# Down projection of a transformer step on one core: two of seven half-size products each replaced by seven quarter-size products

## The chip, the cores and the metric

The kernel runs on one core of one Trainium2 chip, as a single launch. The metric is the device time of one execution in microseconds (us), taken as the median of several runs. Engines are called as the profile calls them: PE (TensorE matmul), PEld (its weight loads), DVE (VectorE), ACT (ScalarE), POOL (GpSimd), and SP (SyncE), which here only issues DMAs. Each engine works its own instructions in the order in which the program lists them.

## The reference

One layer of a streaming encoder with 1024 + 32 frames of width 1024: gated mixers (window attention and short convolution), cross-attention, and a squared-ReLU MLP, then a final norm. The change concerns the last product of the MLP and some sums of its weights:

```
def trunk_layer(x, attn_core, conv_left, mem_k, mem_v, ...):
    h = rms_norm(x, g_mix)
...
    x = x + (jax.nn.sigmoid(ga) * a + jax.nn.sigmoid(gb) * bo) @ w_mix_out
...
    x = x + co @ w_co
    hm = rms_norm(x, g_mlp)
    x = x + jnp.square(jax.nn.relu(hm @ w_up)) @ w_down
    return x, k, v, up[:, -(CONV_WIDTH - 1):]
```

`w_down` is 4096 x 1024, so the down product is 1056 frames x 4096 x 1024.

## The kernel before

All data are float32. A product is made in three matmuls: every operand is split into a rounded part `hi` and a rest `lo`, and PE adds `wh*hi + wh*lo + wl*hi`. A weight tile (128 x 1024, 512 KB) is loaded by SP into a raw buffer `wr`, cast to `wh` by ACT, and `wl = wr - wh` is made by DVE (`split`, `issue_w`). There are two `wr` buffers in the down part of the program and three each of `wh` and `wl`; `next_w` keeps two weights ready beyond the one in use. So the load of a weight can start only when DVE has finished the `wl` of the weight two before it.

Activations lie transposed, 128 features to a tile row. The frames are cut into two halves of 528 (`HT`), each of two quarters of 264 (`QT`). The down product is one level of a Strassen-type scheme: seven half-size products named `b11`, `b21`, `n4`, `t2`, `n3`, `n1`, `b22` in that order (`KINDS`), each 528 frames by 2048 by 512. Their operands (sixteen tiles of 128 x 528 each) were written to DRAM by the up part. `stage` runs one such product as eight items (`steps`, or `paired` for `b11`): an item is one weight tile, half of the depth (8 blocks of 128) for one block of 128 outputs, on both quarters, hence 2 x 8 x 3 = 48 matmuls of 264 columns. After an item, `pump2(3)` splits the operand tiles of the next product that have landed (ACT cast, DVE subtraction in `split_here`, L1319 and L1320) and has SP load three more. When a block of outputs is complete, `to_x1` (L1793) adds it from PSUM to the resident activations `x1`, once for each output quadrant that the product contributes to, in three pieces for each quadrant; for `b11` these are twelve DVE additions.

The sums of weights that Strassen products need (`w_sum`, `g_sum`, the up sums) are made earlier, beside attention: `sum_step` has POOL load a piece of 512 KB, make four additions of 128 x 256 (L735), and store it to DRAM. Two tiles alternate. It works through 50 pieces. Operands marked `pin` keep their program order on an engine; the rest is placed by a scheduler at build time.

Of the kernel before, what the change touches and what calls it, by code (L numbers as in the profile page):

```python
# [40 lines left out]
def hybrid_step(ctx: ExitStack, tc: tile.TileContext, io):  # L41
# [44 lines left out]
    wsum_d = dram.tile([4, 2, 4, P, 4, 256], F32, name="wsum_d")  # L86

# [44 lines left out]
    def weight(key):  # L132
        name, *at = key
        if name in ("w_down", "w_sum"):
            q, j, t = at
            return (wsum_d if name == "w_sum" else io[name])[j, t, :, :, q].rearrange("i p c -> p i c")
        if name == "g_sum":
# [572 lines left out]
    pieces += [("u", i, q) for i in range(2) for q in range(2)]  # L710

# [5 lines left out]

    def sum_step():
        old = W.pop("new", None)
        if pieces:  # L720
            at = pieces.pop(0)
            t = sum_tile(len(pieces))
            if at[0] in ("g", "u"):
                kind, f, q = at
                for e in range(2):
                    src = io["w_in"][34 + 8 * e + f] if kind == "g" else io["w_up"][UP[f][e]]
                    src = src.rearrange("p (h c) -> p h c", h=2)
                    pin(pool_e.dma_start(t[:, 2 * e : 2 * e + 2], src[:, :, 256 * q : 256 * q + 256]))
            else:
                pin(pool_e.dma_start(t, io["w_down"][at]))  # L730
            W["new"] = at, t
        if old:
            at, t = old
            for to, x, y in ((3, 2, 3), (2, 0, 2), (0, 0, 3), (1, 1, 0)):
                pin(pool_e.tensor_tensor(t[:, to], t[:, x], t[:, y], op=ALU.add))  # L735
            if at[0] in ("g", "u"):
                kind, f, q = at
                for w in range(2):
                    pin(pool_e.dma_start((gsum_d[f - 1] if kind == "g" else usum_d[f])[:, w, :, 256 * q : 256 * q + 256], t[:, 2 * w : 2 * w + 2]))
            else:  # L740
                pin(pool_e.dma_start(wsum_d[at], t))
# [9 lines left out]
    for i, h in enumerate(hosts):  # L751
# [14 lines left out]
        if i % 2 and i > 1 or i > 3:  # L766
            extras.append((1, sum_step))
        if h[0] == "Q":
# [475 lines left out]
    def open_first():  # L1244

        closed(m_cm)
        S["l"] = ctx.enter_context(tc.tile_pool(name="first", bufs=4, reuse_waits="tile"))
        S["z"] = ctx.enter_context(tc.tile_pool(name="second", bufs=8, reuse_waits="tile"))
# [7 lines left out]
    def open_sums():  # L1256
        closed(cr_cm)
        closed(Y["cm", 1])
        S["s"] = ctx.enter_context(tc.tile_pool(name="sums", bufs=8, reuse_waits="tile"))
        for kind in ("t2", "n1", "n3", "n4"):  # L1260
            for k in range(4):
                comb[kind, k] = tuple(slot(S["s"], kind, HT) for _ in range(2))
# [11 lines left out]
    def open_second():  # L1274
# [3 lines left out]
        S["b"] = ctx.enter_context(tc.tile_pool(name="b22", bufs=8, reuse_waits="tile", side="right"))  # L1278
        L["cm2"], L["pool2"] = opened("late2", bufs=1, reuse_waits="tile", side="right")
        ps = ctx.enter_context(tc.tile_pool(name="ps2", bufs=1, space=PSUM, reuse_waits="tile"))  # L1280

    def zslot(dt=F32R):
        return S["z"].tile([P, HT], dt, tag="Z", name=nm("Z"))

    def lslot(dt=F32):
        return S["l"].tile([P, HT], dt, tag="lt", name=nm("lt"))
# [102 lines left out]
    def second_b22():  # L1389
        for k in range(4):  # L1390
            comb["b22", k] = tuple(slot(S["b"], "b22", HT) for _ in range(2))
# [212 lines left out]
    KINDS = ["b11", "b21", "n4", "t2", "n3", "n1", "b22"]  # L1604

    def dslots(kind, k):
        if KINDS.index(kind) % 2 == 0:
            tag = ("t2", "n1", "n3", "b22")[k // 4]
            pool = S["b" if tag == "b22" else "s"]
            return tuple(slot(pool, tag, HT) for _ in range(2))  # L1610
        if k < 4:
            return tuple(slot(S["s"], "n4", HT) for _ in range(2))
        if k < 8:
            return tuple(zslot() for _ in range(2))
        if k < 10:
            return tuple(lslot(F32R) for _ in range(2))
        return tuple(slot(S["h"], "H", HT) for _ in range(2))

    def pump2(n):
# [3 lines left out]
        for kind, k in wanted2[:n]:  # L1623
            hi, lo = dn[kind, k] = dslots(kind, k)
            sp.dma_start(lo.bitcast(F32), op_d[kind][:, k])
            coming2.append((hi, lo))
        del wanted2[:n]

    def open_down():
# [3 lines left out]
        S["h"] = ctx.enter_context(tc.tile_pool(name="hpool", bufs=12, reuse_waits="tile"))  # L1633
# [154 lines left out]
    def to_x1(h, f, banks, add=True, last=False):  # L1788
        for c, at, q, frm in SEGS[h]:
# [3 lines left out]
            (dve.tensor_add if add else dve.tensor_sub)(*((x, a, x) if add else (x, x, a)))  # L1793
# [79 lines left out]

    def stage(kind, w, then, q=None, each=None, more=None):
        nxt = KINDS.index(kind) + 1
        if nxt < len(KINDS):
            item(lambda: wanted2.extend((KINDS[nxt], k) for k in range(16)))
        for n, (j, t) in enumerate(paired if kind == "b11" else steps):

            def fn(ws, j=j, t=t):  # L1880
                prod(kind, j, t, then, q)(ws)
                pump2(3)
# [10 lines left out]

    stage("b11", ("w_down", 0), ((*A12, True, False), (*A21, False, False), (*A22, False, False), (*A11, True, False)))
    stage("b21", ("w_down", 1), ((*A11, True, True),))
    stage("n4", ("w_down", 3), ((*A21, True, False),))
# [126 lines left out]
```

## Time and profile before

| | |
|---|---|
| time, median of 3 runs (lowest to highest) | 1748.98 us (1746.13 to 1750.31) |
| span of the profiled execution, first to last instruction | 1747.8 us |
| the execution's own time beyond its span | not recorded apart; the median is 1.2 us above the span |
| mean granted PE clock | 0.995 |
| HBM traffic | 346.60 MB moved, mean 198 GB/s |
| the `b11` product | 1400.6 to 1453.2 us, with the tail of the up part in it |
| the six later down products | 46.8 to 47.8 us each |

The profile gives for each engine the time that it was busy; times count from the first instruction. In a list of waits, a row names who waited, for whom, the total, how often, and the longest. In a table by windows, a row gives for one stretch its length, the busy time of each engine with its count of instructions, the granted clock, the busy share of the DMA engines and the GB/s they moved. In lists of one tile's instructions, three numbers are the shortest, median and longest duration in ns. In a timeline, a row starts with start and duration of a run of instructions of one kind.

### The profile page before, as it was taken

Reading aid. Unit: us, or ns where it says so; the run is one execution under the profiler, and the core shown is the slowest. Engines: PE = TensorE matmul, PEld = TensorE weight load, DVE = VectorE, ACT = ScalarE, POOL = GpSimd, SP = SyncE. Lnnn points to the kernel's source line nnn. Section 1 sums busy time; section 2 is a strip of 40 time slices with the busy share of each in tenths; the row PEclk is TensorE's granted clock in tenths of the full one; section 3 lists DMA queues with packets and bytes.
Section 4 is the critical chain, followed back from the end, with each engine's and each line's share of the span. In section 5 each row is a group of like instructions: output and inputs, shape, how many; then the busy total and the mean of one; then the engine's idle time right before and its main releaser. Section 6 shows DMA issues by size and latency. Waiting matters only on the chain. (4 is left out here: it accounts for less than half of the span.)

```text
span 1747.8 us, 32606 instructions
## 1 busy us (share of the span) xinstructions
PE 1727.7 (99%) x12262; PEld 1712.4 (98%) x12262; DVE 1188.1 (68%) x2276; ACT 852.9 (49%) x1660; POOL 586.2 (34%) x667
## 2 busy tenths in 40 slices
PE   9999999999999999999999999999999999999998
PEld 8999999999999999999999999999999999999998
DVE  7776777768666646555677888787666686545675
ACT  8653534535335324434556666765444463332444
POOL 0026366443553544432224232005555410000121
PEclk9999999999999999999999999999999999999999
DMA  4333344333436888867766667775666695555554
GB/s 185 104 126 128 114 134 153 115 139 127 160 132 204 296 292 280 291 203 238 264 213 198 221 227 241 235 258 191 217 222 219 219 330 185 188 193 169 192 170 160
DMA packets 179854, 346.60 MB, mean 198 GB/s; under 512 B 18657, under 2 KB 101249, under 8 KB 179569
## 3 DMA queue, kind: packets, MB, share of 16 engines
q1 hardware_dynamic: 163504, 290.07, 50.0%
q0 software_dynamic: 15568, 53.68, 8.8%
q8 instruction: 96, 1.57, 0.4%
q10 hardware_dynamic: 624, 0.77, 0.1%
q14 instruction: 62, 0.50, 0.1%
HBM read 250.73 MB, written 93.14 MB: 197 GB/s over the span
## 5 line engine op out<-in xcount | busy, mean ns | idle before, releaser
L129 ACT CAST wh<-wr 128x1024 fp32r<-128x1024 f32 (+1 forms) x214 | 223.8, 1046 | 366.6 <-PE acc L1810 121.4
L130 DVE TENSOR_TENSOR wl<-wr,wh 128x1024 fp32r<-128x1024 f32 (+1 forms) x214 | 275.0, 1285 | 106.2 <-ACT wh L129 105.4
L200 PE MATMUL acc<-X,wh 128*128 128x384 f32 (+1 forms) x864 | 281.5, 326 | 0.0
L201 PE MATMUL acc<-X,wh 128*128 128x384 f32 (+1 forms) x864 | 278.8, 323 | 0.1
L202 PE MATMUL acc<-X,wl 128*128 128x384 f32 (+1 forms) x864 | 277.8, 322 | 0.0
L276 POOL TENSOR_TENSOR xacc<-xacc,ct 128x384 f32<-128x384 f32 (+1 forms) x56 | 75.6, 1354 | 379.9 <-ACT ct L274 378.1
L201 PEld LDWEIGHTS acc<-X,wh 128*128 128x128 f32 x864 | 162.7, 188 | 1.7 <-DVE X L280 0.7
L200 PEld LDWEIGHTS acc<-X,wh 128*128 128x128 f32 x864 | 162.4, 188 | 0.8
L202 PEld LDWEIGHTS acc<-X,wl 128*128 128x128 f32 x864 | 162.4, 188 | 0.1
L200 PE MATMUL acc<-Y,wh 128*128 128x384 f32 (+1 forms) x432 | 139.9, 326 | 3.2 <-DVE ct L1068 2.9
L202 PE MATMUL acc<-Y,wl 128*128 128x384 f32 (+1 forms) x432 | 140.0, 325 | 2.7 <-DMA wl<-wl_d 2.7
L201 PE MATMUL acc<-Y,wh 128*128 128x384 f32 (+1 forms) x432 | 139.7, 324 | 0.0
L129 ACT CAST PTh<-pt 128x512 fp32r<-128x512 f32 (+3 forms) x94 | 45.8, 516 | 112.8 <-PE pt L598 111.4
L1809 PE MATMUL acc<-n,wh 128*128 128x264 f32 x352 | 100.2, 285 | 0.0
L1810 PE MATMUL acc<-n,wh 128*128 128x264 f32 x352 | 100.1, 284 | 0.0
L1811 PE MATMUL acc<-n,wl 128*128 128x264 f32 x352 | 99.9, 284 | 0.0
L735 POOL TENSOR_TENSOR ws<-ws 128x256 f32<-128x256 f32 x100 | 89.5, 895 | 5.6
L735 POOL TENSOR_TENSOR xacc<-xacc 128x256 f32<-128x256 f32 x100 | 86.8, 868 | 5.7 <-DMA xacc<-in_w_in 0.4
L200 PEld LDWEIGHTS acc<-Y,wh 128*128 128x128 f32 x432 | 81.4, 189 | 4.4 <-DVE ct L1068 3.8
L202 PEld LDWEIGHTS acc<-Y,wl 128*128 128x128 f32 x432 | 81.5, 189 | 3.0 <-DMA wl<-wl_d 3.0
L201 PEld LDWEIGHTS acc<-Y,wh 128*128 128x128 f32 x432 | 81.6, 189 | 0.0
L584 ACT ACTIVATE S<-S,nmx 128x257 f32<-128x257 f32 (+1 forms) x132 | 64.2, 488 | 18.9 <-DVE nmx L579 17.6
(432 smaller groups left out, 5554.9 us busy)
## 6 DMA issues: line engine op xcount, KB each, us to landing
wr<-in_w_up SPq DMA_DIRECT2D x53, 512.0 KB, 4.5
wr<-in_w_in SPq DMA_DIRECT2D x52, 512.0 KB, 3.6
wr<-wsum_d SPq DMA_DIRECT2D x40, 512.0 KB, 3.5
wr<-in_w_conv_out SPq DMA_DIRECT2D x24, 512.0 KB, 3.9
wr<-in_w_mix SPq DMA_DIRECT2D x24, 512.0 KB, 5.2
wr<-in_w_down SPq DMA_DIRECT2D x24, 512.0 KB, 3.6
n_d<-Z SPq DMA_DIRECT2D x32, 264.0 KB, 4.2
xacc<-in_w_down POOLq DMA_DIRECT2D x16, 512.0 KB, 4.5
```

The source lines that it names most:

```text
L129: act.copy(hi, src)
L130: dve.tensor_sub(lo, src, hi.bitcast(F32))
L200: pe.matmul(out, wh[:, a], hi, start=(k == 0), stop=False)
L201: pe.matmul(out, wh[:, a], lo, start=False, stop=False)
L202: pe.matmul(out, wl[:, a], hi, start=False, stop=(k == len(acts) - 1))
L276: pool_e.tensor_tensor(acc, acc, sq, op=ALU.add)
L584: act.activation(stl[:, h, : nk + 1], stl[:, h, : nk + 1], AF.Exp, scale=-1.0, bias=nmx[:, h : h + 1], accum_out=den[:, h : h + 1],)
L735: pin(pool_e.tensor_tensor(t[:, to], t[:, x], t[:, y], op=ALU.add))
L1809: pe.matmul(a, wh[:, s], hi, start=(t == 0 and k == 0), stop=False, skip_group_check=True)
L1810: pe.matmul(a, wh[:, s], lo, start=False, stop=False, skip_group_check=True)
L1811: pe.matmul(a, wl[:, s], hi, start=False, stop=(t == 1 and k == 7), skip_group_check=True)
```

## The change

**Products.** `b21` and `n4` no longer run as one half-size product each. `stage2` makes each by seven quarter-size products P1 to P7 (264 frames by 1024 by 256), each as two items, one for each block of 128 outputs, written P1.0 and P1.1. An item is one weight tile and 8 x 3 = 24 matmuls of 264 columns. Before, either product had eight items of 48 matmuls; now it has fourteen of 24, in the program's order P1, P6, P2, P7, P5, P4, P3. Each item needs a weight tile of its own: of `w_down` for P1, P2, P4, and of the new sums `w2_d` for P6, P7, P5, P3. Partial results are kept in three pairs of PSUM banks, which alternate from product to product (`into`), and in plain tiles of SBUF (`wide`): ACT copies P1, DVE adds P1 to P6 and P7, and the outputs of P5, P4, P3 get that sum on DVE and are added to `x1` by POOL.

**Operands.** The sums of operands are made in the stage before (`prepare`): the first eight tiles' quarters (`first_sums` on POOL, `first_split`), and the sums `e` (`extra_split`); in the stage itself those of `f` and the split of the last eight tiles (`second_split2`, three of them with POOL's subtraction). The order of the products becomes b11, b21, t2, n4, n3, n1, b22, and the stages around a `stage2` run in the `paired` order. Each 528-column slot has a fixed place and a list of free places decides which tile goes where.

**Weight sums.** Sixteen pieces are added to `sum_step` (66 instead of 50), with 14 more calls beside attention, and the load of the next piece is issued between the second and the third addition instead of ahead of the first.

```
-    KINDS = ["b11", "b21", "n4", "t2", "n3", "n1", "b22"]
+    KINDS = ["b11", "b21", "t2", "n4", "n3", "n1", "b22"]
+    after2 = [KINDS[KINDS.index(kind) + 1] for kind in RAW2]
...
+    pieces += [("w2", kind, i, b) for kind in RAW2 for i in range(2) for b in range(4)]
...
     def sum_step():
+
         old = W.pop("new", None)
...
+        for n, (to, x, y) in enumerate(((3, 2, 3), (2, 0, 2), (0, 3, 0), (1, 1, 0))):
+            if n == 2 and pieces:
+                sum_load()
+            if old:
+                at, t = old
+                op = ALU.subtract if at[0] == "w2" and to != 3 else ALU.add
+                pin(pool_e.tensor_tensor(t[:, to], t[:, x], t[:, y], op=op))
         if old:
...
+        if i % 2 and i > 4:
+            extras.append((2, sum_step))
...
+        order = ("P1", "P6", "P2", "P7", "P5", "P4", "P3")
+        into = {"P1": "A", "P2": "A", "P6": "B", "P7": "B", "P4": "B", "P5": "C", "P3": "C"}
...
+        def beside(n):
+            if n < 2:
+                last_sums(kind, 2 * n)
+                last_sums(kind, 2 * n + 1)
+            if n < 4:
+                second_split2(kind, 2 * n, False)
+                second_split2(kind, 2 * n + 1, n > 0)
+            elif n < 6:
+                last_split(kind, 2 * n - 8)
+                last_split(kind, 2 * n - 7)
+            if n == 5:
+                wanted2.extend((nxt, k) for k in range(16))
+            if n >= 5:
+                pump2({5: 2, 7: 2, 9: 2, 11: 2, 13: 4}.get(n, 0))
...
-    stage("b21", ("w_down", 1), ((*A11, True, True),))
-    stage("n4", ("w_down", 3), ((*A21, True, False),))
+    stage2("b21", *A11, True)
     stage("t2", ("w_sum", 0), ((*A12, False, False), (*A21, True, False), (*A22, True, False)))
+    stage2("n4", *A21, False)
```

How the instructions now stand is shown at three places, all in the `b21` product.

On DVE, where `b11` ends, this stood before (L1793 is an addition of `b11`'s last block to `x1`, `wl` the rest of a weight, here of the third and fourth of `b21`):

```order
L1793 TENSOR_TENSOR Ga_1727_9917<-acc_3078_17544,Ga_1727_9917 128x264
L1793 TENSOR_TENSOR Ga_1727_9917<-acc_3078_17544,Ga_1727_9917 128x120
L1793 TENSOR_TENSOR Gb_1951_10869<-acc_3078_17544,Gb_1951_10869 128x144
L130 TENSOR_TENSOR wl_17739<-wr_17736,wh_17738 128x1024
L130 TENSOR_TENSOR wl_17803<-wr_17800,wh_17802 128x1024
```

On DVE at the same place after the change (L1907 is that addition, L1713 the split of an operand sum `e`, L1356 that of an operand tile; `wl_17933` is the third weight of `b21`, that of P6.0, and `wl_17978` that of P6.1):

```order
L1907 TENSOR_TENSOR Gb_1967_10999<-acc_3104_17709,Gb_1967_10999 128x144
L1713 TENSOR_TENSOR n_3120_17915<-n_3077_17530,n_3119_17914 128x528
L1713 TENSOR_TENSOR n_3122_17919<-Z_17536,n_3121_17918 128x528
L1713 TENSOR_TENSOR n_3124_17923<-Z_17624,n_3123_17922 128x528
L1713 TENSOR_TENSOR n_3126_17927<-lt_17630,n_3125_17926 128x528
L132 TENSOR_TENSOR wl_17933<-wr_17930,wh_17932 128x1024
L1356 TENSOR_TENSOR H_17350<-H_17350,n_3134_17969 128x528
L1356 TENSOR_TENSOR H_17356<-H_17356,n_3135_17972 128x528
L132 TENSOR_TENSOR wl_17978<-wr_17975,wh_17977 128x1024
```

Four splits of 528 columns moved in between the twelve additions and the next weight, and the weights behind them now serve items of half the length.

On PE and DVE in the middle of the product, after the change. PE first (the last block of P2.0 with weight 18020, then P7.0 with weight 18096; P2.1, whose weight is 18059, starts only after 23 matmuls of P7.0, although the program's order has it ahead):

```order
L2100 MATMUL acc2_3130_17936<-b22_3154_18091,wh_3144_18020 128x264
L2101 MATMUL acc2_3130_17936<-lt_3093_17629,wh_3144_18020 128x264
L2102 MATMUL acc2_3130_17936<-b22_3154_18091,wl_3145_18021 128x264
L2100 MATMUL acc2_3146_18024<-H_3045_17347,wh_3156_18096 128x264
L2101 MATMUL acc2_3146_18024<-H_3046_17348,wh_3156_18096 128x264
L2102 MATMUL acc2_3146_18024<-H_3045_17347,wl_3157_18097 128x264
```

On DVE, the rows from P7.0's weight on (L1907 adds the output of P2.0 and then of P2.1 to `x1`, L1713 splits the sums `f`; the weights are those of P7.0, P7.1, P5.0, P5.1):

```order
L132 TENSOR_TENSOR wl_18097<-wr_18094,wh_18096 128x1024
L1907 TENSOR_TENSOR Ga_1719_9949<-acc_3130_17936,Ga_1719_9949 128x264
L1713 TENSOR_TENSOR b_3159_18126<-n_3132_17963,b_3158_18125 128x528
L1713 TENSOR_TENSOR H_18130<-n_3133_17966,H_18129 128x528
L132 TENSOR_TENSOR wl_18136<-wr_18133,wh_18135 128x1024
L1907 TENSOR_TENSOR Ga_1731_9998<-acc_3130_17936,Ga_1731_9998 128x264
L1713 TENSOR_TENSOR n_3166_18165<-n_3139_18006,H_18164 128x528
L1713 TENSOR_TENSOR Z_18169<-n_3140_18009,n_3167_18168 128x528
L132 TENSOR_TENSOR wl_18181<-wr_18178,wh_18180 128x1024
```

P2.1's addition, which needs the end of P2.1 on PE, stands ahead of P5.0's weight. PE's order of items as built is P1.0, two matmuls of P6.0, P1.1, the rest of P6.0, P6.1, P2.0, P7.0, P2.1, P5.0, P7.1, P5.1, P4.0, P3.0, P4.1, P3.1 (P7.0 and P3.0 leave their last matmul until after P2.1 and P4.1), and the same in `n4`.

On SP near the end of the product, before the change (`wr` are weights, the others operand tiles of the next product):

```order
L159 DMA wr_17670<-in_w_down 128x4x256
L159 DMA wr_17736<-in_w_down 128x4x256
L1625 DMA n_3115_17941<-n_d 128x528
L1625 DMA b_3131_18080<-n_d 128x528
L1625 DMA b_3133_18083<-n_d 128x528
L159 DMA wr_17800<-in_w_down 128x4x256
L1625 DMA b_3135_18086<-n_d 128x528
L159 DMA wr_17873<-in_w_down 128x4x256
```

And after it (the weights are those of P4.1 and P3.0):

```order
L164 DMA wr_18290<-in_w_down 128x4x256
L1670 DMA H_18246<-t_d 128x528
L1670 DMA H_18249<-t_d 128x528
L1670 DMA H_18325<-t_d 128x528
L1670 DMA n_3196_18328<-t_d 128x528
L1670 DMA n_3207_18405<-t_d 128x528
L164 DMA wr_18330<-w_b_105 128x4x256
L1670 DMA Z_18408<-t_d 128x528
L1670 DMA Z_18489<-t_d 128x528
```

Five operand loads now stand in front of P3.0's weight, five more in front of P3.1's, and three in front of the next product's first.

More of the change, by code (lines that the diff above doesn't have):

```diff
@@ L86, in hybrid_step @@
     wsum_d = dram.tile([4, 2, 4, P, 4, 256], F32, name="wsum_d")
+    RAW2 = {"b21": 1, "n4": 3}
+    w2_d = {kind: dram.tile([2, 4, P, 4, 256], F32, name=f"w2_{kind}") for kind in RAW2}
     UP = [(8 * g + i, 8 * g + i + 4) for g in range(4) for i in range(4)]
@@ L718, in sum_step, with sum_store @@
+    def sum_store(at, t):
+        if at[0] in ("g", "u"):
+            kind, f, q = at
+            for w in range(2):
+                to = gsum_d[f - 1] if kind == "g" else usum_d[f]
+                pin(pool_e.dma_start(to[:, w, :, 256 * q : 256 * q + 256], t[:, 2 * w : 2 * w + 2]))
+        elif at[0] == "w2":
+            pin(pool_e.dma_start(w2_d[at[1]][at[2], at[3]], t))
+        else:
+            pin(pool_e.dma_start(wsum_d[at], t))
     def sum_step():
         old = W.pop("new", None)
[L720 to L731, printed above, removed]
@@ L1258, in open_sums @@
         closed(Y["cm", 1])
-        S["s"] = ctx.enter_context(tc.tile_pool(name="sums", bufs=8, reuse_waits="tile"))
+        S["s"] = ctx.enter_context(tc.tile_pool(name="sums", bufs=1, reuse_waits="tile"))
         for kind in ("t2", "n1", "n3", "n4"):
             for k in range(4):
-                comb[kind, k] = tuple(slot(S["s"], kind, HT) for _ in range(2))
+                comb[kind, k] = tuple(at_slot(f"{kind}.{2 * k + i}") for i in range(2))
         for k in range(4):
@@ L1603, in hybrid_step, with take_slot, drop, take_pair @@
     dn, wanted2, coming2 = {}, [], []
-    KINDS = ["b11", "b21", "n4", "t2", "n3", "n1", "b22"]
[L1606 to L1617, printed above, removed]
+    KINDS = ["b11", "b21", "t2", "n4", "n3", "n1", "b22"]
+    after2 = [KINDS[KINDS.index(kind) + 1] for kind in RAW2]
+    places = lambda text: [f"{tag}.{i}" for tag, n in (x.split("*") for x in text.split()) for i in range(int(n))]
+    first_homes = places("t2*8 n1*8 n3*8 b22*8")
+    free = places("H*12 n4*8 Z*8 lt*4")
+    home = {}
+    def take_slot(key, dt=F32R, place=None):
+        assert key not in home
+        home[key] = place or free.pop(0)
+        return at_slot(home[key], dt)
+    def drop(*keys):
+        for key in keys:
+            free.append(home.pop(key))
+    def take_pair(kind, k):
+        own = [first_homes.pop(0) if kind == "b11" else None for _ in range(2)]
+        dn[kind, k] = tuple(take_slot((kind, k, i), place=own[i]) for i in range(2))
+        return dn[kind, k]
+    def drop_pairs(kind, ks):
+        drop(*[(kind, k, i) for k in ks for i in range(2)])
+    def fetch_op(kind, k):
+        hi, lo = take_pair(kind, k)
+        sp.dma_start(lo.bitcast(F32), op_d[kind][:, k])
+        return hi, lo
+    def far_split(hi, lo):
+        raw = lo.bitcast(F32)
+        pin(act.copy(hi, raw))
+        pin(pool_e.tensor_tensor(lo, raw, hi.bitcast(F32), op=ALU.subtract))
     def pump2(n):
@@ L1786, in squares_of, with to_x1 @@
         done[c] += 1
-    def to_x1(h, f, banks, add=True, last=False):
+    def to_x1(h, f, banks, add=True, last=False, eng=None):
         for c, at, q, frm in SEGS[h]:
```

185 lines of the change are left out of this document (161 added, 24 removed).

## The prediction, made before the changed kernel ran

> **What bounds the kernel now.** I read the busy times first, then PE's waits over the whole run, then a table by windows for single down products.
>
> ```profile
> PE 1727.7 (99%) x12262; PEld 1712.4 (98%) x12262; DVE 1188.1 (68%) x2276; ACT 852.9 (49%) x1660; POOL 586.2 (34%) x667
> ...
> PE acc L200 <- DVE ct L1068: 2.9, 3, 1.4
> PE acc L202 <- DMA wl<-wl_d: 2.7, 1, 2.7
> ...
> 1453.20:1500.00 46.80, 46.80 (x387) 46.80 (x387) 26.84 (x45) 18.20 (x27) 3.21 (x2) 1.00 0.58 193
> 1500.00:1546.90 46.90, 46.90 (x387) 46.90 (x386) 22.77 (x36) 17.36 (x25) 1.57 (x1) 1.00 0.54 178
> ```
>
> PE is the bound: busy 99% of the span, and no entry of its list of waits is above 2.9 us. In the two windows, which are `b21` and `n4`, PE never pauses and the clock is full. DVE works 27 and 23 us of 47, ACT 18 and 17, the DMA engines 58% and 54%. So matmuls taken away shorten the time one for one, and every pause put into PE lengthens it one for one.
>
> **The gain.** Each product has 384 matmuls (8 items of 48), and 46.9 us / 384 = 0.122 us for one. Fourteen items of 24 are 336. So 48 fewer in each, 96 in all, and 96 x 0.122 = 11.7 us. An item lasts 24 x 0.122 = 2.93 us instead of 5.86.
>
> [...]
>
> **What it costs: weights in half the time.** In these windows a weight is loaded, cast and split as follows (timeline of ACT and of DVE, then all weights after `b11`):
>
> ```profile
> 1511.81 1.05 ACT L129 CAST wh<-wr 128x1024 fp32r<-128x1024 f32 x1 [3.21 <-issue]
> 1513.30 1.16 ACT L1319 CAST Z<-Z 128x528 fp32r<-128x528 f32 x2
> ...
> 1512.65 1.93 DVE L1320 TENSOR_TENSOR n<-n,n 128x528 fp32r<-128x528 f32 x3
> 1514.50 1.22 DVE L130 TENSOR_TENSOR wl<-wr,wh 128x1024 fp32r<-128x1024 f32 x1
> ...
> L130 DVE TENSOR_TENSOR wl<-wr,wh x54: 1211/1225/1668, 1456.4 to 1729.9; 128x1024 fp32r<-128x1024 f32 x54
>   PE acc L1810: 121.0, 31
> DMA to landing us min/median/max: 3.4/3.5/6.4
> ```
>
> A cast takes 1.05 us, the subtraction 1.22, a load 3.4 to 3.5 when nothing is ahead of it. The loads use two raw buffers, so the turn of one buffer is 3.45 + 1.05 + 1.22 and about 0.1 for hand-overs, 5.8 us, and it must serve one item in two. Before, two items were 11.7 us and half of that turn was slack (ACT's wait for PE, 121.0 us in 31 cases, is that slack). Now two items are 5.86 us: the turn just fits, with nothing left for an operand load in the queue or for another instruction ahead on ACT or DVE. Where it doesn't fit, PE waits. DVE's sum alone wouldn't bound: 14 x 1.22 for weights, about 20 x 0.62 for operand splits and 12 additions of about 0.4 are 34 us of 41. It is the order that costs. I walk through `b21`, time zero being the start of P1.0, each wait in its turn.
>
> ```profile
> 1447.63 0.84 DVE L1793 TENSOR_TENSOR Ga<-acc,Ga 128x240 f32<-128x240 f32 x3 [3.26 <-PE acc L1811]
> ...
> 1450.62 0.70 DVE L1320 TENSOR_TENSOR H<-H,H 128x528 fp32r<-128x528 f32 x1
> 1451.23 1.23 DVE L130 TENSOR_TENSOR wl<-wr,wh 128x1024 fp32r<-128x1024 f32 x1
> 1453.45 0.84 DVE L1793 TENSOR_TENSOR Gb<-acc,Gb 128x240 f32<-128x240 f32 x3 [1.00 <-PE acc L1811]
> ...
> 1456.44 1.22 DVE L130 TENSOR_TENSOR wl<-wr,wh 128x1024 fp32r<-128x1024 f32 x1
> ```
>
> (1) `b11`'s twelve additions take 2.99 us (1447.63 to 1450.62); those of its last-but-one block begin at -5.62. Now four splits (1.93 / 3, so 0.62 each with overlap, 2.46), P1.1's weight (1.22), the last twelve additions (2.99), four more splits (2.46) and then P6.0's weight (1.22) follow: -5.62 + 2.99 + 2.46 + 1.2 + 2.99 + 2.46 + 1.22 = 7.7. PE is at the third matmul of P6.0 at 2 x 2.93 + 0.24 = 6.1. **Wait 1.6.** Before, the same weight was done at 1457.7, 4.4 us into the product, and needed after 11.7. In `n4` the stage ahead has nine additions for a block, not twelve, and DVE waits for the block's end: 0.2 + 2.3 (9/12 of 2.99) + 2.46 + 1.22 = 6.2, **wait 0.1**. Bounds 0 to 2.5.
>
> (2) P2.0's weight takes P6.0's buffer: issued at 7.7, landed 11.2 to 11.5, cast and split by 13.8; PE needs it at 13.6. P2.1's weight lands at 13.6, and ACT's casts of the last two operand tiles stand behind its cast: 14.7, 15.8; DVE's split of the tile is done at 16.9, after the weight and an addition. P2.0 needs it with its 20th matmul, at 15.9. **Wait 0.2 + 1.0** in each product; bounds 0 to 2.
>
> (3) P7.0 now stands ahead of P2.1. Its raw buffer came free at 13.8, so landed 17.3, cast 18.4, split 19.65. P2.0 ends at 17.55 and P7.0's third matmul is due at 17.8. **Wait 1.9**, bounds 0 to 3.
>
> (4) P2.1 then ends at 25.2. Its addition stands on DVE ahead of two splits and P5.0's weight: 25.2 + 0.2 + 0.35 + 1.23 + 1.22 = 28.2. PE reaches P5.0's third matmul at 25.3 + 0.24. **Wait 2.6**, bounds 0 (the addition is the only cause) to 3.5.
>
> (5) P7.1, P5.1 and P4.0 have their weights in time. P3.0's weight is issued near 34, behind five operand loads. SP's timeline has such a burst, and the landing of its last weight follows:
>
> ```profile
> 1438.41 0.38 SPq L159 DMA_DIRECT2D wr<-in_w_down  x1
> 1439.33 1.27 SPq L1625 DMA_DIRECT2D t<-n_d  x3
> 1440.80 0.79 SPq L1625 DMA_DIRECT2D n<-n_d  x2
> 1441.68 0.38 SPq L159 DMA_DIRECT2D wr<-in_w_down  x1
> ...
> DMA to landing us min/median/max: 6.7/6.7/6.7
> ...
> 1400.60:1420.00 19.40, 19.40 (x161) 19.40 (x160) 16.35 (x23) 12.26 (x20) 6.17 (x4) 1.00 1.03 366
> ```
>
> The weight behind five loads took 6.7 us. At the rate of saturated engines (366 GB/s in the last row) five loads of 0.27 MB and a weight of 0.52 MB need 5.1 us, and the first starts 2 us (3.4 less 1.4 of transfer) after its issue near 31.3, so landing lies between 38.5 and 40.7, the weight is split between 40.8 and 43, and P3.0's third matmul is due at 39.9. P3.1's weight, behind five more, and the next product's first, behind three, come within about a microsecond of their turn. **Wait 1.8** together, the low side of 1 to 5, since the row of 6.7 also had the end of the up part in its queue.
>
> Sum: `b21` 1.6 + 1.2 + 1.9 + 2.6 + 1.8 = 9.1; `n4` 0.1 + 1.2 + 1.9 + 2.6 + 1.8 = 7.6; together 16.7, against the gain of 11.7. That is +5.0 us. On the span it gives 1752.8; the median is 1.2 us above the span, which I add: 1754.0.
>
> **What costs nothing.** The stages `b11` and `t2` split the same sixteen tiles as before in other pieces, and POOL's 24 subtractions there fall where POOL is idle (1.57 of 46.9 us in the window above); cover: two items of 5.86 us between load and use; bound 0 to 2, since `t2`'s second and third weights also stand behind five and six loads. Beside attention, POOL gets 64 additions and 48 DMA issues more:
>
> ```profile
> 200.00:300.00 100.00, 100.00 (x647) 98.62 (x646) 69.64 (x173) 40.16 (x97) 54.61 (x79) 1.00 0.39 127
> ...
> L735 POOL TENSOR_TENSOR xacc<-xacc 128x256 f32<-128x256 f32 x88 | 77.4, 880 | 4.9 <-DMA xacc<-in_w_in 0.4
> ...
> L728 POOL DMA_DIRECT2D ws<-in_w_in x14 | 10.4, 744 | 7.3 <-DMA gsum_d<-ws 6.8 <-issue 0.5
> ...
> L730 POOL DMA_DIRECT2D xacc<-in_w_down x15 | 8.3, 552 | 45.8 <-DMA wsum_d<-xacc 44.6 <-issue 1.1
> ```
>
> 64 x 0.88 + 48 x 0.74 = 92 us over some 450 us raise POOL from 55% to about 75% there, while PE is busy without a gap. The load moved between additions gives its buffer's store 1.8 us more to land, and POOL's 44.6 us of waiting at that place will shrink; PE waits for none of it now, so that is worth nothing. If a convolution's multiplication comes late behind a sum, PE loses up to its own wait: bound 0 to 3.
>
> **Rivals.** *The turn keeps up* (faster). If a lone load takes 3.4 and ACT and DVE are free when they are wanted, waits (2), (3) and (5) fall to nothing, P2.1's addition comes early and (4) goes too; (1) stays, and perhaps 1 us in each product: 1.7 + 2 = 3.7 lost, 1754.0 - 16.7 + 3.7 = 1741.0. For it: the turn of 5.8 against 5.86. Against it: sixteen operand loads share the queue. It decides at a turn of 5.9 us. *Bursts bound* (much slower): each weight behind five loads takes the 6.7 us of the row, 3.2 over a lone load, twice in each product: 4 x 3.2 = 13 in place of the 3.6 in (5), so 1754.0 + 9.2 = 1763. For it: that row. Against it: the early half of each product has few loads. *Late POOL beside attention*: up to 3 us, with (3) or (4) half as large, about 1752. *The change doesn't do what it says*: the built program has 96 matmuls fewer, so this has no chance.
>
> **How the numbers follow.** My forecast, 1746 to 1759 (waits of 9 to 22), has 0.52, of which 0.32 lies above 1752.5; the turn that keeps up 0.25; the bursts 0.15; late POOL 0.08. A measurement of this kernel tells 0.2%, 3.5 us, from no change: faster means under 1745.5, slower above 1752.5. Faster 0.25, within 0.20 + 0.08 = 0.28, slower 0.32 + 0.15 = 0.47. With every wait at its lower bound the time would be 1739, with every one at its upper bound 1774, neither likely; for 8 in 10 I take 1740.5 to 1764, the rivals' own times. The forecast's own range is 1746 to 1759.
>
> **What would show it.** Right: 11,900 or so matmuls at the same pace; PE's list of waits with entries for `wl` of the weights and for an operand split, 1 to 3 us each, some five in each product, and `b21` and `n4` at 48 to 50 us instead of 46.9. (1) shows as a wait near 6 us after `b11`, (4) as one for the weight's split right after P2.1, (5) as landing times of 5 to 7 us. Wrong: windows of 41 to 43 us for both products with no such waits; or waits before 700 us, which would put the cost into the sums beside attention.

## The result and the profile after

The changed kernel takes **1794.43 us** (median of 5 runs, 1791.42 to 1795.82) against 1748.98 before: ratio 1.0262, 95% interval 1.0243 to 1.0280, so 45 us slower. The prediction said slower, but 1754.0, with a forecast range of 1746 to 1759 and 8 chances in 10 up to 1764. The profiled run took 1795.82 us with a span of 1794.0.

The busy times of the changed kernel, and the table by windows for the stages of down. For comparison I add the windows of `b11` and `t2` before, which the prediction didn't show (columns: window, its length, busy time and count of PE, of its weight loads, of DVE, ACT and POOL, then the granted clock, the DMA engines' busy share and GB/s).

```profile
PE 1741.9 (97%) x12166; PEld 1716.5 (96%) x12166; DVE 1269.9 (71%) x2322; ACT 881.9 (49%) x1716; POOL 756.5 (42%) x869
```

```profile
1408.70:1470.90 62.20, 56.31 (x434) 55.26 (x433) 47.87 (x84) 28.77 (x51) 32.12 (x31) 0.95 0.66 231
1470.90:1528.90 58.00, 47.68 (x338) 45.84 (x337) 40.47 (x59) 26.05 (x38) 16.86 (x18) 0.91 0.64 206
1528.90:1580.50 51.60, 49.61 (x386) 48.56 (x385) 40.31 (x66) 23.69 (x43) 31.66 (x32) 0.97 0.47 163
1580.50:1638.00 57.50, 47.92 (x339) 45.97 (x338) 42.13 (x56) 25.16 (x35) 17.20 (x17) 0.91 0.67 212
1638.00:1687.10 49.10, 48.21 (x386) 47.05 (x386) 32.41 (x52) 22.96 (x35) 5.02 (x5) 1.00 0.66 220
```

```profile
1400.60:1453.20 52.60, 52.60 (x434) 52.60 (x433) 43.52 (x82) 28.07 (x43) 6.17 (x4) 1.00 0.88 305
1546.90:1593.70 46.80, 46.80 (x387) 46.80 (x386) 27.06 (x54) 16.93 (x24) 0.00 (x0) 1.00 0.55 184
```

The five rows of after are `b11`, `b21`, `t2`, `n4`, `n3`; the two rows of before are `b11` and `t2`. The 96 matmuls are gone as predicted (12166 for 12262; the "11,900 or so" among the prediction's signs doesn't fit its own 96). But PE pauses: it is busy 47.7 of 58.0 us in `b21`. Against 336 x 0.122 = 41.0, `b21` loses 17.0 and `n4` 16.5; `b11` loses 9.6, `t2` 4.8, `n3` 2.2 (46.9 before); and down begins at 1408.7 where it began at 1400.6, so 8.1 were lost ahead of it. Less the gain of 11.7 that is 46.5, the 46.2 by which the spans differ. So the loss has three parts: **ahead of down, in the stages beside the products, and in the products.** PE's waits from the start of `b21` to the end of `n4`, `t2` between them included (engine, line, what it waited for: total, times, longest):

```profile
PE acc L2102 <- DVE wl L132: 12.1, 7, 3.2
PE acc L2100 <- ACT wh L131: 2.7, 2, 1.4
PE acc L2101 <- DVE Z L1356: 1.8, 2, 1.1
PE acc L2100 <- DVE ct L2058: 1.7, 2, 0.8
```

L2100 to L2102 are the products' matmuls. Most of it is `wl`, the weight's second half, which DVE makes last; then `wh`, its cast on ACT, and the split of an operand (L1356). The last row is of another kind, and so are two smaller ones with L2053, of 0.6 each: L2058 and L2053 are additions that read a result from PSUM, and the second item of a product waits until the first item's result has been read.

A second thing shows in PE's timeline, here at a wait in `b11` (start, duration; in brackets the idle time ahead and what ended it):

```profile
1440.94 0.28 PE L1924 MATMUL acc<-t,wh 128*128 128x264 f32 x1
1445.28 0.59 PE L1925 MATMUL acc<-t,wl 128*128 128x264 f32 x1 [4.05 <-DVE wl L132]
1445.66 0.43 PE L1923 MATMUL acc<-t,wh 128*128 128x264 f32 x1
1445.88 0.43 PE L1924 MATMUL acc<-t,wh 128*128 128x264 f32 x1
...
1450.50 0.29 PE L1924 MATMUL acc<-t,wh 128*128 128x264 f32 x1
1450.63 0.29 PE L1925 MATMUL acc<-t,wl 128*128 128x264 f32 x1
```

Before the pause matmuls start 0.12 us apart, after it 0.22 for some 5 us, then 0.12 again. In `b21` and `n4` such slow stretches hold 5.1 us more than the same matmuls at full pace; the other 12.0 and 11.3 us are the pauses themselves. The granted clock shows it: 0.50 in a window from 1445 to 1450 us, and on average 0.91 in the rows of the two products above. The prediction had no term for it.

### The profile page after: what moved, and what is told of

Same layout as the page of the kernel before. It is cut to its first block, busy times and chain, and to the rows that moved or that the text cites. A ratio compares the mean times of both kernels' runs of the same rounds, so it can differ in the third digit from the quotient of the medians.

```text
span 1794.0 us, 32861 instructions
## 1 busy us (share of the span) xinstructions
PE 1741.9 (97%) x12166; PEld 1716.5 (96%) x12166; DVE 1269.9 (71%) x2322; ACT 881.9 (49%) x1716; POOL 756.5 (42%) x869
## 3 DMA queue, kind: packets, MB, share of 16 engines
q1 hardware_dynamic: 169840, 296.37, 49.7%
## 5 line engine op out<-in xcount | busy, mean ns | idle before, releaser
L131 ACT CAST wh<-wr 128x1024 fp32r<-128x1024 f32 (+1 forms) x226 | 236.1, 1045 | 360.9 <-PE acc L206 80.8
L132 DVE TENSOR_TENSOR wl<-wr,wh 128x1024 fp32r<-128x1024 f32 (+1 forms) x226 | 303.5, 1344 | 108.7 <-ACT wh L131 107.5
L762 POOL TENSOR_TENSOR xacc<-xacc 128x256 f32<-128x256 f32 x132 | 115.0, 871 | 29.4 <-DMA xacc<-in_w_down 22.4
L762 POOL TENSOR_TENSOR ws<-ws 128x256 f32<-128x256 f32 x132 | 111.2, 842 | 26.6 <-DMA ws<-in_w_down 19.0
L905 PE MATMUL acc<-n,wh 128*128 128x264 f32 x256 | 72.9, 285 | 1.0 <-DVE Z L1572 1.0
L907 PE MATMUL acc<-n,wl 128*128 128x264 f32 x256 | 73.1, 285 | 0.0
L906 PE MATMUL acc<-n,wh 128*128 128x264 f32 x256 | 72.9, 285 | 0.0
```

What stands on the lines that cost most here:

```text
L131: act.copy(hi, src)
L132: dve.tensor_sub(lo, src, hi.bitcast(F32))
L762: pin(pool_e.tensor_tensor(t[:, to], t[:, x], t[:, y], op=op))
L905: pe.matmul(acc, wh[:, a], hi, start=(start and k == 0), stop=False, skip_group_check=True)
L906: pe.matmul(acc, wh[:, a], lo, start=False, stop=False, skip_group_check=True)
L907: pe.matmul(acc, wl[:, a], hi, start=False, stop=(k == 3), skip_group_check=True)
```

## The experiments

Times are medians; a ratio is to the kernel before, run beside it, with its 95% interval. One per mille is 1.75 us. A single trace of these kernels stands up to 11 us off its own median, so sizes go by the ratios, and the traces say only where.

### Ahead of down: the sums and the fixed places

**e1: the sums alone in the kernel before.**

```diff
+    pieces += [("w2", kind, i, b) for kind in RAW2 for i in range(2) for b in range(4)]
+        if i % 2 and i > 4:
+            extras.append((2, sum_step))
+            if n == 2 and pieces:
+                sum_load()
```

> The kernel before with nothing but the sums' part of the change: sixteen more weight sums beside attention, the load between the second and the third addition, fourteen more calls; the sixteen new sums are stored and not used. In the trace after the change, down starts 8.1 us later than before (1408.7 against 1400.6). Theory A, the sums put 8 us into attention and what follows: 1757. Theory B, the sums cost nothing in the end (in the trace after, PE is at matmul 5600 0.3 us earlier than before) and the 8 us come from the slots that are now fixed places: 1749, within 2 us of before.

1752.45, ratio 1.0029 (1.0011 to 1.0047): 2 to 8 us. Neither theory is met; the sums cost some, and something else is missing.

**g1: the fixed places alone** (both products as before, sums as before, a third raw buffer so that the next group's effect is out of it), **and g2: the third raw buffer alone in the kernel before.**

```diff
     def open_down():
...
+        third.update(n=0, pool=W["pool"])
```

> f1_old_raw3 with the sums of the kernel before (no sixteen more, load first, fewer calls): fixed places and a third raw buffer alone. f1 stands 4.6 to 11 us above before. Theory M, that is the sums beside attention (e1 alone was 2 to 8 above before): 1750 to 1752. Theory N, places cost as much as the sums, in the stretch at 1070 to 1220 us where e1 lost nothing: 1754 to 1756.

> The kernel before with the third raw buffer in down and nothing else. The kernel before has no wait for a weight in down, so all theories say 1749 within 2 us; if it is faster, the gain of e8 and f1 is in part one that the kernel before could have had too.

g1: 1749.66, 1.0009 (0.9997 to 1.0022). g2: 1746.65, 0.9994 (0.9983 to 1.0006). Places cost next to nothing ahead of down, theory M; and a third buffer was no gain in the kernel before, where no weight is late.

**h1: the new order of load and additions alone; h2: the sixteen more sums with the old order.**

```diff
-            if n == 2 and pieces:
+            if n == 0 and pieces:
                 sum_load()
```

> The kernel before with the load of the next weight sum moved between the second and the third addition, and neither the sixteen more sums nor the fourteen more calls. e1 (all three) is 2 to 8 us above before, g1 (neither) within 0.5 under and 4 over. Theory R, the order costs: POOL now waits for a store between its additions and holds convolutions up: 1751 to 1755. Theory S, the number of sums costs: within 1.5 us of before.

> The kernel before with the sixteen more sums and the fourteen more calls, but the load ahead of all four additions as before. Theory R: within 1.5 us of before, since only the order costs. Theory S: 1751 to 1755, as e1 or worse, since POOL also waits longer at its loads.

h1: 1749.82, 1.0022 (1.0005 to 1.0039). h2: **1766.06, 1.0115** (1.0098 to 1.0131), far above the 1751 to 1755 written down. So the sixteen sums cost some 20 us in the old order, and the new order wins back some 15 of them. PE's longest wait beside the sums in h2, then the end of the chain that led to it (start, duration), and two of POOL's waits at the loads of the new sums:

```profile
PE acc L202 <- ACT wh L131: 10.7, 1, 10.7
```

```profile
800.10 7.07 DMA w_n<-ws
...
817.21 1.01 POOL ct L1091
...
819.17 0.96 ACT wh L131
```

```profile
POOL ws L734 <- DMA w_b<-ws: 20.4, 4, 5.2
POOL ws L734 <- DMA w_n<-ws: 17.8, 3, 7.2
```

With the load first, POOL must wait until its own earlier store has left the tile before it may load into it. Over the run these waits are 124 us in the kernel before, where PE has no wait of over 2.7 us, 205 in h2 and 80 in e1; in e1 another 63 us of waiting for the loads to land stand in their place. What is new in h2 is 65 us at the loads of the new sums (`w_b`, `w_n`). So POOL works on them until 816 us, and its first addition of the convolution's output (L1091) starts at 817.2, where it started at 802.1 before. ACT stands 18.8 us waiting for that addition, and the cast of the weight that PE needs comes behind it. PE loses 14 us between matmul 4800 and 5200 (749 to 814 us in the kernel before), 10.7 of them in that one wait.

### Both products undone: what the places cost in b11

**e2: fixed places and sums kept, both products as before; e5: e2 with the places handed out in the old order; f1: e2 with a third raw buffer.**

```diff
-    stage2("b21", *A11, True)
+    stage("b21", ("w_down", 1), ((*A11, True, True),))
+    stage("n4", ("w_down", 3), ((*A21, True, False),))
...
-    stage2("n4", *A21, False)
```

```diff
-    free = places("H*12 n4*8 Z*8 lt*4")
+    free = places("n4*8 Z*8 lt*4 H*12")
```

> The changed kernel with the two products b21 and n4 computed as before (eight full items each), in the order b11, b21, n4, t2; the sums and the fixed places stay. Theory A and B above agree that the part before down is as in the changed kernel, so down starts at 1408 to 1409 and the time is 1757, with no wait of PE over 1 us in b21, n4 and t2. If instead the 8 us before down were a matter of chance between executions, the time would be 1749.

> e2_old_products (both products as before, sums and fixed places kept) with one line changed: the places of the second operand are handed out in the order of the kernel before (n4, Z, lt, H) and no longer H first. Theory A, b11's loss comes from the order of places: H is free first, so SP issues the next operand's loads ahead of b11's third and fourth weight while the DMA engines are saturated (five more loads stand between the second and the third weight in e2): the 7 us that e2 lost in b11 go to below 1, the time from 1765 to about 1758. Theory B, b11's loss is the drift of a later start of down: no change, 1762 to 1768.

> e2_old_products (both products as before, sums and fixed places kept) with the third raw buffer of e8. Theory I, b11's loss in e2 and e5 (4 to 7 us, on the third and fourth weight) is a weight load that starts too late for its item, behind operand loads that fixed places let go earlier: the third buffer starts it earlier, b11 is within 1 us of 48 and the time is 1756 to 1760. Theory J, b11's loss has to do with the places alone: 1763 to 1768.

e2: 1764.99, 1.0088 (1.0058 to 1.0117). e5: 1767.12, 1.0100 (1.0066 to 1.0134). f1: 1757.49, 1.0045 (1.0026 to 1.0064). e2 lies above its 1757, with no wait in `b21`, `n4`, `t2`: what it loses within down is all in `b11`. The order of the places (theory A) is not its cause: e5 loses it too. The third buffer removes it (theory I). The windows of `b11` in e2, e5 and f1 (392, 381 and 392 matmuls):

```profile
1419.60:1474.10 54.50, 50.69 (x392) 49.97 (x392) 39.31 (x71) 27.64 (x43) 6.08 (x4) 0.94 0.88 303
```

```profile
1408.00:1460.20 52.20, 48.42 (x381) 47.91 (x380) 38.83 (x68) 26.97 (x42) 6.19 (x4) 0.97 0.87 304
```

```profile
1408.40:1456.00 47.60, 47.60 (x392) 47.59 (x391) 39.14 (x71) 27.50 (x43) 6.14 (x4) 1.00 0.93 323
```

SP's queue shows why. A place of its own is free as soon as its last reader is done, so the next operand's loads go out earlier, ahead of `b11`'s fifth weight: in the changed kernel eleven transfers stand between the fourth and the fifth weight, in the kernel before six. Eleven stand in every run with the places, in e2 and e5 ahead of the fifth weight, in f1, e8 and g1, with a third buffer, only ahead of the sixth. In e1, which has the sums without the places, there are six, and `b11` loses 0.9 us. That piece of the queue, its first rows and its last, after and before:

```profile
1423.32 0.38 SPq L164 DMA_DIRECT2D wr<-in_w_down  x1
1423.75 0.51 SPq L1695 DMA_DIRECT2D n<-b_d  x1
...
1431.99 0.43 SPq L164 DMA_DIRECT2D wr<-in_w_down  x1
```

```profile
1414.98 0.38 SPq L159 DMA_DIRECT2D wr<-in_w_down  x1
1415.62 0.32 SPq L1625 DMA_DIRECT2D H<-b_d  x1
...
1419.98 0.71 SPq L159 DMA_DIRECT2D wr<-in_w_down  x1
```

From the fourth weight's load to the fifth's it is 8.7 us instead of 5.0, with the DMA engines full (a share of 1.04 to 1.06 from 1420 to 1440 us in the changed kernel). The fifth weight lands at 1438.2, so its split stands behind the additions of a block that PE ends at 1440.8, and starts at 1444.0: that is the wait of 4.05 us in PE's timeline above.

### Inside the products

**e4: only b21 in quarter-size products.**

```diff
-    stage2("n4", *A21, False)
+    stage("n4", ("w_down", 3), ((*A21, True, False),))
```

> The changed kernel with b21 in quarter-size products and n4 as before. If each product's loss is its own, n4 and what it puts on t2 and n3 go away: 57.5 - 46.9 = 10.6, 4.7 and 2.2, so 1794 - 17.5 = 1777. If a loss in b21 is partly made up or passed on later, the time is 1783 or more.

1787.08, 1.0219 (1.0192 to 1.0246). Its trace is 14.0 us shorter than that of the changed kernel and has none of the losses in `n4` and behind it, but it was the fastest of four runs; by the medians the second product costs 7 us, not 17.5, which is the other theory (1783 or more). The other three runs left no trace, so the size stays open.

**e6: PE kept busy in its waits** with idle matmuls into a spare bank.

```diff
+        FILL = {("P6", 0, 2): {"b21": 20, "n4": 14}, ("P2", 0, 19): 5, ("P5", 0, 2): 18, ("P3", 0, 2): 6}
...
+                            for _ in range(many[kind] if isinstance(many, dict) else many):
+                                pin(pe.matmul(z, *x, start=True, stop=True, skip_group_check=True))
```

> The changed kernel with PE kept busy where it waits in b21 and n4: idle matmuls into a spare bank (20 and 14 ahead of the third matmul of P6.0, 5 in P2.0, 18 ahead of the third of P5.0, 6 ahead of that of P3.0; 0.122 us each, all shorter than the wait at their place). Theory C, the slow stretches (matmuls 0.22 us apart, 5.1 us in each product) follow from PE's pauses of over 2 us: the pauses are filled, the slow stretches fall to below 2 us in each product, the weights come no later, the time falls by 6 to 9, to 1785 to 1789. Theory D, the clock is slow for another reason (the power of the whole stage, or the DMA): the slow stretches stay at 5 us, the time stays at 1794 or rises.

1797.04, 1.0262 (1.0232 to 1.0292). The windows of `b21` and `n4` in e6:

```profile
1474.70:1531.10 56.40, 49.18 (x388) 47.33 (x387) 39.95 (x59) 26.03 (x38) 16.13 (x18) 1.00 0.67 215
...
1582.20:1641.30 59.10, 51.11 (x381) 49.44 (x380) 41.07 (x56) 25.20 (x35) 16.95 (x17) 0.94 0.64 205
```

Half of each theory. The slow stretches do follow from the pauses: filled, `b21` has a clock of 1.00 for 0.91 and about 1 us of slow matmuls for 5. But the product takes 56.4 us for 58.0, `n4` takes 59.1 for 57.5 with a new pause of 3.2, and the kernel is no faster; the intervals leave room for a gain of some 6 us at most. So not all of the 10 us of slow clock is a cost of its own here, and perhaps none. The likely reason is that while PE is slow, the next weight comes closer, and a faster PE only waits longer for it: something other than PE would then give the pace.

**e7: P2's additions put off** behind item P5.1.

```diff
             elif p == "P2":
-                out(i, 0, 0, a, dve)
+                put_off.append(lambda: out(i, 0, 0, a, "late"))
...
+                    if n == 9:
+                        for x in put_off:
+                            x()
```

> The changed kernel with the additions of P2.0 and P2.1 put off on DVE behind item P5.1, so that P5.0's weight no longer stands behind the addition of P2.1 (step 4 of the prediction). Theory E, step 4 is as predicted: the wait of 2.69 us at the third matmul of P5.0 falls below 0.5 in both products, and the slow stretch behind it goes: 1786 to 1789. Theory F, the loads bound the second half of the product anyway: the wait goes but those at P4.1, P3.0 and P3.1 grow by as much: 1792 to 1795.

1793.49, 1.0242 (1.0210 to 1.0275): theory F by the median, though the interval takes in theory E's range too. The wait at P5.0 fell from 2.7 to 0.2 in both products, as step 4 has it, but P5.1 now waits 1.4 in both, half of it for its weight, and P3.0 in `n4` 3.7 where it was 2.5. The products take 56.6 and 56.8 us instead of 58.0 and 57.5.

**e8: a third raw buffer in down** (the line of g1, in the changed kernel).

> The changed kernel with a third raw buffer for weights in down (a tile that nothing else uses there), so that a load may start one item earlier. Theory G, the turn of two raw buffers is what makes weights late at P6.1, P2.0, P7.0 and P3 (steps 2, 3 and 5 of the prediction, 6.0 us of waits in b21 as measured): these fall to 2 us or less, and b11's late weights come earlier too: 1780 to 1786. Theory H, ACT's and DVE's order sets those waits: 1792 to 1796.

**1773.35, 1.0127** (1.0099 to 1.0154): 21 us of the 45 are gone, more than theory G's 1780 to 1786. `b11` takes 55.0 us for 62.2, and `b21` with `t2` 101.3 for 109.6:

```profile
1405.70:1460.70 55.00, 53.47 (x434) 52.84 (x433) 51.16 (x84) 28.80 (x51) 33.52 (x31) 1.00 0.75 262
1460.70:1562.00 101.30, 92.98 (x723) 91.29 (x722) 83.77 (x124) 49.97 (x80) 48.53 (x49) 0.97 0.60 201
```

What gives the pace is the turn of the two raw buffers, and the trace of the changed kernel shows it closed: loads of SP, casts of ACT and subtractions of DVE in `b21`.

```profile
1474.19 0.37 SPq L164 DMA_DIRECT2D wr<-w_b  x1
...
1480.78 0.37 SPq L164 DMA_DIRECT2D wr<-in_w_down  x1
...
1484.27 0.37 SPq L164 DMA_DIRECT2D wr<-in_w_down  x1
```

```profile
1477.70 1.04 ACT L131 CAST wh<-wr 128x1024 fp32r<-128x1024 f32 x1 [2.24 <-DMA wr<-w_b]
```

```profile
1479.54 1.21 DVE L132 TENSOR_TENSOR wl<-wr,wh 128x1024 fp32r<-128x1024 f32 x1
1480.67 2.44 DVE L1356 TENSOR_TENSOR H<-H,n 128x528 fp32r<-128x528 f32 x2
1483.03 1.21 DVE L132 TENSOR_TENSOR wl<-wr,wh 128x1024 fp32r<-128x1024 f32 x1
```

A subtraction ends at 1480.75 and a load starts at 1480.78; the next ends at 1484.24 and a load starts at 1484.27. The weight loaded from 1474.19 is cast at 1477.70, but DVE, behind in its queue, subtracts it only at 1483.03: a turn of 10.0 us. Of the eleven loads from 1480.78 on, ten start within 0.03 us of such an end. Over twelve weights, the first loaded from 1474.19 and the last, which is already `t2`'s, from 1517.66, the turn is 7.8 us on average (load 4.55, ACT late 0.25, cast 1.05, DVE late 0.70, most of it at two of the twelve, subtraction 1.27), and 8.0 in `n4`. With two buffers that is one weight in 3.9 to 4.0 us, and fourteen weights make 55 to 56 us, nearly the length of the products (58.0 and 57.5). The loads' part of it, from the view of the loads' line for these twelve:

```profile
DMA to landing us min/median/max: 3.4/4.3/7.0
```

**f3: e8 and e7 together; f4: f3, and the additions of the last block of b11 and t2 put off** behind P6.0.

```diff
+                if kind in ("b11", "t2") and j == 3:
+                    put_off2.append(outs)
+                else:
+                    outs()
...
+                    if n == 2:
+                        put_off2.pop()("late")
```

> e8_raw3 with P2's additions put off as in e7. In e7 the wait of 2.69 us at P5.0 went (0.21) and later waits on the weights' casts took its place. Theory K, that was the turn of two raw buffers; with a third one the 2.7 us at P5.0 are won in both products, and the slow stretch behind each (1.6 us) too: 1773 - 5.4 - 3.2 = 1765, 1763 to 1769. Theory L2, DVE's and ACT's work bounds the products with three buffers as well: 1771 to 1775.

> f3_raw3_defer, and the twelve (nine) additions of the last block of b11 (t2) put off on DVE behind P6.0 (step 1 of the prediction). If step 1 stands and the loads no longer bind, the waits at P6.0 (2.5 and 1.5 us in e8) fall below 0.5 and a slow stretch of 1.6 us goes: 4 to 6 us below f3, 1758 to 1764. If the additions only move to another wait, within 2 us of f3.

f3: 1768.11, 1.0102 (1.0069 to 1.0134), within theory K's 1763 to 1769: what moved to other waits with two buffers seems to be won with three. Only the traces say so: from the changed kernel to e7 the two products lose 2.1 us together, from e8 to f3 11.9 (53.9 and 56.7 become 49.7 and 49.0). By the ratios it is 3.5 and 4.4, neither clear of noise. f4: 1767.82, 1.0093 (1.0056 to 1.0130), no difference: the wait at P6.0 fell from 2.5 to 1.8 in `b21` and from 1.5 to 1.0 in `n4`, and behind it in `b21` stand waits of 2.7 and 2.1 where f3 has one of 0.5.

### POOL beside DVE

**e3: the operands' sums on POOL left out of the changed kernel (the raw tiles are split in their place, as many splits as before); f5: the same out of f4; g3: f4 with these sums on DVE.**

```diff
-        pin(pool_e.tensor_tensor(t3, quarter(x1_, 1), quarter(x0, 1), op=ALU.subtract))
-        pin(pool_e.tensor_tensor(quarter(r, 0), t3, quarter(x0, 0), op=ALU.add))
-        pin(pool_e.tensor_tensor(quarter(r, 1), quarter(x1_, 0), quarter(r, 0), op=ALU.subtract))
```

> The changed kernel without POOL's 24 + 8 additions and subtractions of operands in each of the two preparations (first sums and last sums are left out; raw tiles are split in their place). Theory P, POOL's instructions slow those of DVE beside them (a split of 528 columns took 1.2 to 1.3 us beside POOL, 0.7 alone) and so make the weights late: b11 falls from 62.2 to 55 or less, the wait at P6.0 from 3.3 to about 1.6 in b21, the time to 1775 to 1784. Theory L, the loads and the turn of two raw buffers set the waits, as the prediction has it: the time stays within 3 us of 1794.

> f4_raw3_defer2 without POOL's first and last sums of operands (left out as in e3). Theory P, the sums slow DVE's splits beside them (1.25 us for 0.70) and so hold up operands and weights in b11, t2 and at the start of both products: 4 to 8 us below f4. If DVE has room with three buffers, within 2 us of f4.

> f4_raw3_defer2 with the first and last sums of operands on DVE and no longer on POOL. f5, which leaves them out, is 8 to 9 us faster than f4. Theory P2, what costs is that both engines work on the same operands at once (a split 1.25 us for 0.70): 32 sums of 0.4 us on DVE, 13 us of its time per product, cost less than that, 1760 to 1766. Theory Q, DVE has no room: the weights stand behind the sums, 1768 to 1780.

e3: 1786.86, 1.0231 (1.0197 to 1.0266), between the two theories, and its interval doesn't tell it from the changed kernel. f5: 1759.11, 1.0043 (1.0021 to 1.0064), 9 us below f4, a little more than the 4 to 8 written down. g3: 1774.69, 1.0155 (1.0139 to 1.0172), theory Q; by its trace DVE lacks room in `b21` (58.4 us, with waits of 5.3 and 3.5), not in `b11` and `t2`, which take 52.8 and 46.8. The price on POOL shows in `t2` of the changed kernel, DVE above and POOL below at the same time:

```profile
1542.68 1.25 DVE L1356 TENSOR_TENSOR H<-H,b 128x528 fp32r<-128x528 f32 x1
1543.86 1.77 DVE L132 TENSOR_TENSOR wl<-wr,wh 128x1024 fp32r<-128x1024 f32 x1
```

```profile
1537.38 0.75 POOL L1702 TENSOR_TENSOR n<-ct,t 128x264 f32<-128x264 f32 x1
...
1541.10 1.09 POOL L1702 TENSOR_TENSOR n<-ct,n 128x264 f32<-128x264 f32 x1
```

A split takes 1.25 us where it takes 0.70 alone, a weight 1.77 for 1.22, and POOL's sum beside a split 1.1 to 1.2 for 0.75 (the first POOL row, when DVE was idle). So DVE's busy time in `t2` falls from 41.9 to 33.9 us with the sums gone, for 66 and 67 instructions; the rows of f4 and f5:

```profile
1518.50:1565.30 46.80, 46.80 (x386) 46.80 (x385) 41.93 (x66) 24.89 (x45) 31.93 (x32) 1.00 0.56 194
1508.00:1554.80 46.80, 46.80 (x386) 46.80 (x385) 33.86 (x67) 24.77 (x45) 5.61 (x5) 1.00 0.54 187
```

In e3, without the sums, the wait at P6.0 is 1.1 us in `b21` and none in `n4`; in the changed kernel 3.3 and 2.3. In `t2` of the changed kernel both engines work at one pace: from 1539.1 to 1543.9 us DVE starts an instruction every 1.18 us, and from 1539.8 to 1543.3 POOL starts one every 1.18 on average, a little under the 1.45 that a split and a sum take one after the other when each is alone. By what one engine holds up the other no run shows. Leaving the sums out also takes away the splits' waiting for them and the places that they hold; how much of the 9 us is the shared pace alone no run tells.

## Why the prediction was wrong

**The gain** was right: 96 matmuls, 0.122 us each.

**What failed first is the sentence that the turn of the raw buffers "just fits"** at 5.8 us. It took the durations of a quiet stage of the kernel before. Measured it is 7.8, since loads land in 4.55 on average beside the operands' loads (3.45 assumed), and a subtraction on DVE stands 0.7 behind others and takes 1.27 on average for 1.22 (beside POOL in `t2` 1.77). At 7.8, above the 5.86 of two items, the turn doesn't make a few waits of known size; it sets the pace of the whole product, and a third buffer, which takes this bound away, wins 21 of the 45 us (e8). The prediction named the point itself ("It decides at a turn of 5.9 us"), but only as the bound of its faster rival. Its sum for DVE, 34 us of 41 in a product, was short too: the rows of `b21` and `n4` show 40.5 and 42.1, so DVE had no slack to come back from a delay.

**The waits one by one** were seen in the right places. Time from one matmul's start to the next less 0.12, in us, `b21` / `n4`:

```
step                         predicted    after       without POOL's sums (e3)
(1) P6.0, weight             1.6 / 0.1    3.3 / 2.3   1.1 / 0.0
(2) P2.0, weight, operand    1.2 / 1.2    0.9 / 1.2   1.7 / 1.3
(3) P7.0, weight             1.9 / 1.9    0.3 / 0.2   1.1 / 0.6
(4) P5.0, weight             2.6 / 2.6    2.7 / 2.7   2.7 / 2.7
(5) P3.0, weight             1.8 / 1.8    2.4 / 2.5   1.0 / 3.1
P5.1, addition, weight       -            0.0 / 0.0   1.4 / 1.4
P1.1, P6.1, P3.1, reading    -            2.2 / 2.3   2.0 / 2.0
```

- Step 1's mechanism holds (DVE's backlog at the end of `b11`); its size was off, because four splits and a weight took 6.0 us beside POOL's sums (1468.2 to 1474.2) where 3.7 were counted. e3 gives the predicted size.
- Step 2's operand wait came as computed. Step 3's wait was mostly swallowed, since PE reached P7.0 late; in e3, with less lost at P6.0, it is 1.1 and 0.6.
- Step 4 was exact, and e7 and f3 show the cause is P2.1's addition. But alone it is worth nothing that is clear of noise (e7): by the trace, with two buffers later weights become late in its place.
- Step 5 was 0.6 short of what P3.0 waited; loads behind the bursts landed in 5 to 7 us, as it said.
- Missing were the second items: P1.1, P6.1 and P3.1 wait until the copy or addition has read the first item's result. Both items write to one PSUM tile, each to its own half; whether the chip or the program's own ordering asks for this wait no run shows. It was in no term.

The five steps come to 18.5 us in both products where 16.7 were predicted, but that is luck: step 1 was 3.9 too small and step 3 was 3.3 too large. With the second items all pauses are 23.4, above the 9 to 22 given. And the sum was wrong in kind: with two buffers the waits aren't separate terms, they share one pace. Removing one (e7), or filling it (e6), moved it.

**"What costs nothing" cost most.** The stages beside the products, bounded at 0 to 2, lost 16.6. In `b11` some 7 us come from the fixed places, which the prediction took as bookkeeping: they let loads overtake weights (e2, e5, f1). The rest and `t2` come with POOL's sums beside DVE, by the waits in the trace: f5 puts all of these sums at 9 us with three buffers, e3 at some 5 with two, which is not clear of noise. The prediction looked only at whether POOL was idle, not at whom it would slow. The sums beside attention, bounded at 0 to 3, cost about 5 (e1), and the moved load, said to be worth nothing since PE waited for none of POOL's waits, is worth some 15 once the new sums are there (h2): it keeps them from holding up the work on POOL that PE needs.

**The slow clock** was not foreseen, 10 us of the two products by the trace. e6 shows that it follows from the pauses; filling them won nothing that was measured, and some 6 us at the most.

By ratios the 45 us are then, in the order in which they were taken away: two raw buffers 24 (after against e8, 7 of them in `b11`), P2.1's addition 4 (e8 against f3, not clear of noise; f4's step can't be told from nothing), operand sums on POOL 9 (f4 against f5), and sums beside attention and places 8 (f1). In another order the shares may differ: POOL's sums were some 5 with two buffers (e3). What f5 has left over f1 is nothing, so the gain of 11.7 is still eaten there by waits of about 11 us at its two products and the starts of the stages behind: in its trace `b21` and `n4` take 46.8 us each, as in the kernel before. No version here beats the kernel before. Open are e4's size, and whether the new order alone costs anything (h1's interval begins at 1 us above before, its trace is 2 us below).

## What to carry to other kernels

A product with half the work for a weight needs twice the weights in the same time: compute the turn of a buffer from mean durations in the busy stage, not from those of a quiet one, and where it exceeds its share, take one weight per turn and buffer as the pace; here a buffer more was worth more than any other single change. When a change gives tiles places of their own, read the new order of the load queue, since a load that may start earlier is also in front of something. And work that is moved to an idle engine is to be priced by what it does to its neighbour (here a split of 0.70 us took 1.25): one run without it tells.

## What the runs showed of the hardware

In the changed kernel PE's granted clock dropped to half after some pauses and stayed there for 3 to 5 us (matmuls 0.22 us apart for 0.12; 0.50 in the window from 1445 to 1450 us, 0.91 over `b21` and over `n4`). From one matmul's start to the next, the pauses ahead of such stretches were 4.3 us in `b11`, 3.5 and 2.4 at P6.0, 2.8 at P5.0 in both products, and at P3.0 two close together, of 1.6 or 1.7 and of 1.0; in `t2` there were four, of 0.4, 0.8, 0.8 and 1.1, within 4.4 us. But the length alone doesn't tell: in the kernel before, PE's idle time of 1.87 us that ended at 669.6 us had a clock of 0.53 behind it (window from 671 to 674 us), and in the changed kernel another of 1.87 us, which ended at 1000.0, had the full clock (1.00 from 1000 to 1005 us). Nor did four pauses close together always slow it: in `b11` there were four of 0.6 to 0.8 within 5.3 us, and the clock stayed at 1.00 (window from 1426.3 to 1432 us). What decides it no run here shows.
